# Gated linear attention on Trainium2: score strips of 32 x 32 in place of 64 x 64 for the diagonal and five levels

## The chip, the cores and the metric

The kernel runs on one core of one Trainium2 chip. The metric is the device time of one execution in microseconds (us). Times of a kernel are the median of several executions; the profile comes from one more execution with its own time.

The engines are named as the profile names them: PE (TensorE's matmuls), PEld (TensorE's weight loads), DVE (VectorE), ACT (ScalarE), POOL (GpSimd) and SP (SyncE, which here issues DMAs).

## The reference, cut to what matters

The program is a two-layer backbone over 1024 latent tokens and 256 context tokens. The first layer has neighbourhood attention and mLSTM heads; the second has 16 heads of gated linear attention, run forwards and backwards over the tokens. The change is in the second layer. What one direction of one head computes is, for chunks of the sequence:

```python
b = jnp.cumsum(lfc, axis=2)                       # logs of the decays, per key dimension
o = jnp.einsum('bhtk,bhkv->bhtv', qc * jnp.exp(b), S)
pair = jnp.exp(jnp.where(tri, b[:, :, :, None, :] - b[:, :, None, :, :], -jnp.inf))
a = jnp.einsum('bhtk,bhtsk->bhts', qc, pair * kc[:, :, None, :, :])
o = o + jnp.einsum('bhts,bhsv->bhtv', a, vc)
S = jnp.exp(bL[:, :, 0])[..., None] * S + jnp.einsum('bhsk,bhsv->bhkv', kc * jnp.exp(bL - b), vc)
```

The score `a` of a query t and a key s is a sum over 128 key dimensions, each with its own product of decays between s and t. Layer outputs are normalized per head, gated and projected.

## The kernel before

The kernel has stages in this order: the first layer's input projections, attention, mLSTM and output projection; then the second layer's projections; then from about 2170 to 3165 us the 16 heads, one after another; then the output projection.

**The scores of a head.** The kernel cuts the 1024 tokens into 8 blocks of 128 and computes the scores inside a block for both directions together, into one matrix A of 128 keys by 128 queries a block (`gA`, [128, 8, 128]). It works up through levels. At level `lev` (0 to 6, with h = 2^lev) pairs of neighbouring groups of h tokens meet: keys of one group with queries of the other. `gK` and `gQ` hold keys and queries, each in two copies for the two directions, multiplied with the decays up to the edge of their present group; `gF` (later `gT`) holds each group's total decay. Per level, in `hg_level` (L1450 to L1495):

- ACT copies the right half of each pair's keys out of `gK` into `gksel` (L1466), which has one buffer;
- DVE multiplies `gK` with the neighbour's total decay (`update(K, ...)`, the multiply at L1461);
- PE computes the level's products (L1431, through `strip`);
- DVE multiplies `gQ` in the same way (L1461), and then the totals of two groups into one (L1488);
- the product is merged into the running scores `gD`.

**Strips.** A product isn't made for the whole block of 128 by 128. Up to level 5 a pair of groups lies within 64 tokens, so only the two 64 x 64 squares on a block's diagonal hold anything. `strip` (L1429) computes one of them: all 128 key dimensions, 64 keys as the stationary operand in half of the array's columns (`tile_position=(0, b * 64)`), 64 queries moving. A level has 16 strips, two for each of the 8 blocks. The operands are fp32, and the trace shows each strip as two weight loads and two matmuls. Results are [128, 8, 64] in a PSUM bank (tag `s`, four buffers in this stage).

**Merging.** The diagonal's strips (in `hg_intra`, products of `gkn` and `gq`) are multiplied by a mask into `gD` ([128, 8, 64], L1406). Levels 0 to 5 are merged by a predicated copy under the level's mask (`self.lmask`, L1490). Level 6 joins the two halves of a block; ACT then copies the `gD` squares into A's diagonal squares (L1494) and level 6's result into the other two (L1495). `hg_scan` (L1527 to L1529) uses A with the values.

**What else runs between the levels.** PE fills the time between the trains of strips with the projection of the head's values and gates (`hg_vz`, the dense products of L131 to L133 into `mm`), the transposes of the previous head's output (`hg_out`, L1580), and the context's state (`hg_ctx`: DVE at L1351 to L1357, PE at L1362 and L1372).

**What sets the order.** The kernel is written in program order and a planner with a simulated timeline orders each engine's instructions. `urgent()` gives the level's steps priority over the rest. `seg()` makes PE's pieces follow one another as written (`issue_after(self.last_pe.ins)`), so PE's order is fixed by hand; DVE's and ACT's order is the planner's. Weights come on SP's queue, outputs and sums of weights on POOL's; neither is part of a level's steps.

Elsewhere in the kernel two products use narrow columns of the array as well: the modulation's (L265 and L175: four strips of 32 columns with 512 moving) and neighbourhood attention's (L889: two of 64).

Of the kernel before, what the change touches and what calls it, by code (L numbers as in the profile page):

```python
# [10 lines left out]
F32 = mybir.dt.float32  # L11
F32R = mybir.dt.float32r
U8 = mybir.dt.uint8
AF = mybir.ActivationFunctionType
ALU = mybir.AluOpType
# [4 lines left out]
P = 128  # L20
D = 1024
KD = D // P
LAT = 1024
CTX = 256
SQ = 256
T = LAT + CTX
NT = T // P
# [18 lines left out]
class Prog:  # L46
# [1336 lines left out]
    def hg_intra(self, h, st, pool, prev):  # L1383
        nc = self.nc
        F, q = st["F"], st["q"]
        K = self.t(pool, [P, 2, LAT], F32, "gK", 1)
        nc.vector.tensor_scalar(out=K, in0=F, scalar1=-1.0, scalar2=1.0, op0=ALU.mult, op1=ALU.add)
        if h == 0:
            self.Q = self.t(pool, [P, 2, LAT], F32, "gQ", 1)
        Q = self.Q  # L1390
        ks = [self.t(pool, [P, 512], F32, "gkn", 4) for _ in range(2)]
        halves = [(hf, slice(hf * 512, (hf + 1) * 512)) for hf in (1, 0)]
        with self.urgent():
            for hf, s in halves:
                nc.vector.tensor_tensor(out=ks[hf], in0=K[:, 0, s], in1=K[:, 1, s], op=ALU.add)
            for hf, s in halves:
                for d in range(2):
                    nc.vector.tensor_tensor(out=Q[:, 1 - d, s], in0=q[hf], in1=F[:, d, s], op=ALU.mult)
        hv = dict(Q=Q, K=K, T=F, D=self.t(pool, [P, 8, 64], F32, "gD", 1))
        pa = self.ps("s", [P, 8, 64])  # L1400
        with self.urgent(), self.seg():
            for c in range(8):
                for b in range(2):
                    o = c % 4 * P + b * 64
                    m = self.strip(pa[:, c, :], b, ks[c // 4][:, o : o + 64], q[c // 4][:, o : o + 64])
        nc.vector.tensor_tensor(  # L1406
            out=hv["D"], in0=pa, in1=self.lmask[:, 0, :].unsqueeze(1).to_broadcast([P, 8, 64]), op=ALU.mult
        )
        self.last_pe = m
        tiles = self.hg_vz(st, pool)  # L1410
        for lev in range(7):
            if lev == 6:
                hv["A"] = self.t(pool, [P, 8, P], F32, "gA", 1)
            self.hg_level(hv, lev, pool)
            if lev in (1, 2) and prev:
                prev(lev)
            if lev == 3:
                ctx = self.hg_ctx(st, pool)
                next(ctx)
            if lev == 4:  # L1420
                S = next(ctx)
                if prev:
                    prev(3)
            next(tiles)
        next(tiles)
        return hv, S


    def strip(self, out, b, lhsT, rhs):  # L1429
        s = slice(b * 64, (b + 1) * 64)  # L1430
        return self.nc.tensor.matmul(out[s], lhsT=lhsT, rhs=rhs, start=True, stop=True, tile_position=(0, b * 64))  # L1431


    def hg_close(self, H, hf, pool):
# [14 lines left out]
    def hg_level(self, H, lev, pool):  # L1449
        nc = self.nc  # L1450
        n, h = LAT, 1 << lev
        nb = n // (2 * h)
        K, Q, A, D, Tt = H["K"], H["Q"], H.get("A"), H["D"], H["T"]

        pick = lambda t: _skew(t[:, 0, :].rearrange("p (b s i) -> p b s i", s=2, i=h), 2, n)
        out = self.ps("s", [P, 8, 64])

        def update(t, o, step):
            v = bass.AP(t.tensor, t.offset, [list(t.ap[0]), [n + h, 2], [2 * h, nb], [1, h]])
            tot = bass.AP(Tt.tensor, Tt.offset + o, [list(Tt.ap[0]), [step, 2], [2, nb], [0, h]])  # L1460
            nc.vector.tensor_tensor(out=v, in0=v, in1=tot, op=ALU.mult)  # L1461

        with self.urgent():
            if lev < 6:
                ksel = self.t(pool, [P, n], F32, "gksel", 1)
                m = nc.scalar.copy(ksel.rearrange("p (b s i) -> p b s i", s=2, i=h), pick(K))  # L1466
                if lev == 5:
                    self.level = m
                update(K, 1, n - 1)
            for c, b in ((c, b) for c in range(8) for b in range(2)):  # L1470
                with self.seg():
                    o = c * P + b * 64
                    r = out[:, c, :]
                    if lev < 6:
                        r = r.rearrange("p (b s i) -> p b s i", s=2, i=h)
                        lhsT, rhs = ksel[:, o : o + 64], pick(Q)[:, o // (2 * h) : (o + 64) // (2 * h)]
                    else:
                        lhsT = K[:, b, o : o + 64]
                        rhs = Q[:, 1 - b, c * P + (1 - b) * 64 : c * P + (2 - b) * 64]
                    run = self.strip(r, b, lhsT, rhs)  # L1480
            self.last_pe = run
            update(Q, n + 1, -n - 1)
            if lev == 6:
                update(K, 1, n - 1)
            Tv = Tt[:, :, 0 : 2 * nb].rearrange("p d (b s) -> p d b s", s=2)
            if lev == 6:
                H["T"] = self.t(pool, [P, 2, nb], F32, "gT", 1)
            nc.vector.tensor_tensor(out=H["T"][:, :, 0:nb], in0=Tv[:, :, :, 0], in1=Tv[:, :, :, 1], op=ALU.mult)  # L1488
        if lev < 6:
            nc.vector.copy_predicated(D, self.lmask[:, lev + 1, :].unsqueeze(1).to_broadcast([P, 8, 64]), out)  # L1490
            return
        for b in range(2):
            s, e = slice(b * 64, (b + 1) * 64), slice((1 - b) * 64, (2 - b) * 64)
            nc.scalar.copy(A[s, :, s], D[s])  # L1494
            nc.scalar.copy(A[s, :, e], out[s])  # L1495

    def hg_states(self, st, H, d, c0, c1):
        v = st["v"]
# [98 lines left out]
    def build(self):  # L1597
        tc, nc, a = self.tc, self.nc, self.a
        dma = nc.sync.dma_start
        with ExitStack() as es:  # L1600
# [25 lines left out]
            def load(name, shape, eng=nc.gpsimd):  # L1626
# [12 lines left out]
                out=self.hnc[:, 1, :], in0=self.hnc[:, 0, :], scalar1=-1.0, scalar2=None, op0=ALU.mult  # L1639
# [5 lines left out]
                out=self.qkn, in0=qkn[:, 0:1], scalar1=qkn[:, 1:2], scalar2=0.125, op0=ALU.mult, op1=ALU.mult  # L1645
# [11 lines left out]
            for i in range(2):  # L1657
# [6 lines left out]
                out=self.lb[:, 1, :], in0=self.lb[:, 0, :], scalar1=-1.0, scalar2=1.0, op0=ALU.mult, op1=ALU.add  # L1664
# [16 lines left out]
            with self.pp.phase(ad=2, e=2), tc.tile_pool(name="pre", bufs=2) as pool:  # L1681
# [64 lines left out]
                for t0 in range(4, NT, 2):  # L1746
                    mod(t0, t0 + 2)
                    if t0 == 6:
                        hm, lm = self.h_last
# [75 lines left out]
            lk = self.fp = l1.enter_context(tc.tile_pool(name="hgk", bufs=1))  # L1825
            self.ntw = 1
            with tc.tile_pool(name="op0", bufs=2) as op, ExitStack() as wl:
# [14 lines left out]
                    later = later[2:]  # L1842
                self.zero = self.t(lk, [P, CTX], F32, "gzero", 1)
                nc.vector.memset(self.zero, 0.0)
                self.lmask = self.t(lk, [P, 7, 64], U8, "glm8", 1)
                lm = self.t(op, [P, D], F32, "nx", 1)[:, 0 : 7 * P].rearrange("p (l f) -> p l f", f=P)
                dma(out=lm, in_=a["glm"])
                for b in range(2):
                    s = slice(b * 64, (b + 1) * 64)
                    nc.vector.tensor_copy(self.lmask[s, 0, :], self.ident[s, s])  # L1850
                    nc.vector.tensor_copy(self.lmask[s, 1:7, :], lm[s, 0:6, s])
                self.gate_bc(0, op, 2, 0)
                ys = [self.out_y(4, q, self.yd, op, 4) for q in range(2)]
                wr.close()
# [31 lines left out]
            with l1:  # L1886
# [20 lines left out]
                with tc.tile_pool(name="sx", bufs=1, side="right", reuse_waits="tile") as tp, self.pp.phase(x=4):  # L1907
# [4 lines left out]
                pool, wzp, wv, st = pools  # L1912
                pool = _Two(
                    pool, wzp, l1.enter_context(tc.tile_pool(name="hg", bufs=2, reuse_waits="tile")),
                    ("gq", "gK", "gQ", "gkn", "gksel"), ("wzl", "wzh"),
                )
                for t, n, f in (
                    ("gv", 2, NT * P), ("gz", 1, LAT), ("gEc", 1, 2 * CTX), ("gD", 1, 512), ("gknc", 1, 512), ("gS0", 8, P), ("gS1", 8, P),
                    ("gA", 1, LAT), ("gF", 1, 2 * LAT), ("gFc", 1, 2 * CTX), ("wraw", 3, 512), ("gyt", 1, 512),
                    ("gss", 2, 4), ("gT", 1, 16),  # L1920
                ):
                    for _ in range(n):
                        self.t(pool, [P, f], F32, t, n)
# [62 lines left out]
                for i, k in enumerate((0, 4)):  # L1986
                    raw8 = self.t(pool, [P, 512], F32, "wraw", 3)
                    dma(
                        out=raw8.rearrange("p (j t) -> p j t", j=4),
# [5 lines left out]
                w = block(W[0:D, 0:512], wr * 4 + wo * 4, None, ([pool, 3, "wraw"],) * 7 + ([pool, 1, "gyt"],))  # L1995
# [4 lines left out]
                w = block(self.sw[1], wo * 4 + wr * 4)  # L2000
# [46 lines left out]
            with tc.tile_pool(name="op1", bufs=2) as op, ExitStack() as wl, tc.issue_after(w5_dma.ins):  # L2047
# [26 lines left out]
                e = self.t(wl1, [P, 4, 512], F32, "oe", 1)  # L2074
# [137 lines left out]
def _skew(ap, dim, extra):  # L2212
    a = [list(x) for x in ap.ap]
    a[dim][0] += extra
    return bass.AP(ap.tensor, ap.offset, a)
# [90 lines left out]
```

## Time and profile before

| | us |
|---|---|
| median of three runs | 3311.36 |
| lowest and highest | 3306.84, 3313.35 |
| the profiled execution | 3313.05 |
| its span, first to last instruction | 3311.3 |

| engine | busy, us | share of the span |
|---|---|---|
| PE | 3252.1 | 98% |
| PEld | 2899.0 | 88% |
| DVE | 2217.8 | 67% |
| ACT | 1456.0 | 44% |
| POOL | 797.7 | 24% |

In the trace a row of the timeline is: start, duration, engine, line, operation, the tile written and those read, shape (partitions x elements, for PE active rows * columns ahead of it), the number of instructions merged into the row, and in brackets the idle time ahead of it with what ended it. A row of several matmuls lasts from the first start to the last end. Rows of groups give minimum, median and maximum duration in ns, or the busy time and the mean. The list of waits says who waited for whom: us in total, times, the longest. The share of an engine over the whole span is a mean over stages; here only the stage of the heads matters.

### The profile page before, as it was taken

The page shows a single profiled execution, that of the slowest core. Times are in us where ns is not written, and L with a number is a line of the kernel's source. Part 1 is how long each engine was busy: PE and PEld are TensorE (multiplying, and loading weights), DVE is VectorE, ACT ScalarE, POOL GpSimd, SP SyncE. Part 2 cuts the span into 40 slices and gives each one's busy share as a digit, 9 for nine tenths or more (in the row PEclk, how much of TensorE's full clock was granted, in tenths as well). Part 3 has the DMA queues.
Part 4 walks back from the last instruction along what each step waited for, and adds up shares of the span by engine and source line. Part 5 has one row for each costly group of instructions (what it writes and reads, how often), then busy time and mean ns, then how long its engine had stood idle before and what let it go on. Part 6 is the DMA issues. An engine that isn't in the chain of part 4 may idle for free.

```text
span 3311.3 us, 64736 instructions
## 1 busy us (share of the span) xinstructions
PE 3252.1 (98%) x24746; PEld 2899.0 (88%) x24746; DVE 2217.8 (67%) x5005; ACT 1456.0 (44%) x3396; POOL 797.7 (24%) x1191
## 2 busy tenths in 40 slices
PE   7999999999999999999999999999999999999999
PEld 6799899988989888898878788899999999999977
DVE  5847666666655566687767755577778678677756
ACT  5245554455544444455446333333433433433443
POOL 2222222222211112211110233312332333333210
PEclk9999999999999999999999999999999999999999
DMA  7713222232233434444653233322322324334376
GB/s 238 259 50 86 86 71 81 68 94 84 73 90 103 145 111 123 131 139 147 204 175 114 94 105 105 99 80 76 115 83 92 115 83 111 94 86 103 91 218 167
DMA packets 338103, 379.81 MB, mean 115 GB/s; under 512 B 34601, under 2 KB 269801, under 8 KB 336769
## 3 DMA queue, kind: packets, MB, share of 16 engines
q1 hardware_dynamic: 286032, 236.73, 24.3%
q0 software_dynamic: 51760, 138.94, 13.4%
q8 instruction: 195, 3.19, 0.4%
q14 instruction: 116, 0.94, 0.1%
HBM read 272.31 MB, written 103.08 MB: 113 GB/s over the span
## 4 chain that ended last, share of the span: by engine, by line
PE 82%; DMA 6%; issue 4%; DVE 4%; ACT 2%; POOL 1%; SPq 1%; POOLq 0%; ACTq 0%; DVEq 0%
PE mm L131 15%; PE mm L132 15%; PE mm L133 15%; PE s L1431 4%; PE acc L889 2%; PE tr L869 2%; PE x L131 2%; PE x L132 2%; PE x L133 2%; PE mm L951 2%; PE mm L953 2%; PE acc L661 2%; PE mm L952 2%; PE s L670 2%; PE s L1502 1%
## 5 line engine op out<-in xcount | busy, mean ns | idle before, releaser
L131 PE MATMUL mm<-wh,hh 128*128 128x256 f32 (+1 forms) x1440 | 445.6, 310 | 2.9 <-ACT wh L73 0.8
L132 PE MATMUL mm<-wl,hh 128*128 128x256 f32 (+1 forms) x1440 | 444.9, 309 | 0.0
L133 PE MATMUL mm<-wh,hl 128*128 128x256 f32 (+1 forms) x1440 | 442.3, 307 | 0.0
L131 PE MATMUL mm<-hh,wh 128*128 128x512 f32 (+1 forms) x1076 | 391.2, 364 | 2.7 <-ACT ev L399 1.6
L132 PE MATMUL mm<-hl,wh 128*128 128x512 f32 (+1 forms) x1076 | 387.1, 360 | 0.7 <-DVE hl L346 0.7
L133 PE MATMUL mm<-hh,wl 128*128 128x512 f32 (+1 forms) x1076 | 386.6, 360 | 0.0
L131 PE MATMUL mm<-wzh,hh 128*128 128x256 f32 x1024 | 294.4, 287 | 0.0
L131 PEld LDWEIGHTS mm<-wh,hh 128*128 128x128 f32 x1440 | 271.5, 189 | 17.4 <-issue 1.0
L133 PE MATMUL mm<-wzh,hl 128*128 128x256 f32 x1024 | 284.0, 277 | 0.0
L132 PE MATMUL mm<-wzl,hh 128*128 128x256 f32 x1024 | 283.9, 277 | 0.0
L132 PEld LDWEIGHTS mm<-wl,hh 128*128 128x128 f32 x1440 | 271.4, 188 | 12.6 <-issue 0.7
L133 PEld LDWEIGHTS mm<-wh,hl 128*128 128x128 f32 x1440 | 271.4, 188 | 11.9 <-issue 0.5
L131 PEld LDWEIGHTS mm<-hh,wh 128*128 128x128 f32 x1076 | 202.7, 188 | 32.8 <-ACT ev L399 3.7
L133 PEld LDWEIGHTS mm<-hh,wl 128*128 128x128 f32 x1076 | 202.3, 188 | 29.8 <-DVE wl L74 0.2
L132 PEld LDWEIGHTS mm<-hl,wh 128*128 128x128 f32 x1076 | 202.8, 188 | 28.6 <-DVE hl L346 1.4
L131 PEld LDWEIGHTS mm<-wzh,hh 128*128 128x128 f32 x1024 | 192.8, 188 | 2.4
L132 PEld LDWEIGHTS mm<-wzl,hh 128*128 128x128 f32 x1024 | 192.7, 188 | 0.0
L133 PEld LDWEIGHTS mm<-wzh,hl 128*128 128x128 f32 x1024 | 192.4, 188 | 0.0
L74 DVE TENSOR_TENSOR wl<-wraw,wh 128x512 fp32r<-128x512 f32 x174 | 118.4, 688 | 60.2 <-ACT wh L73 58.2
L1461 DVE TENSOR_TENSOR gQ<-gQ,gF 128x1024 f32<-128x1024 f32 x112 | 142.5, 1272 | 19.3 <-PE s L1431 19.3
L1466 ACT COPY gksel<-gK 128x1024 f32<-128x1024 f32 x96 | 110.5, 1151 | 100.0 <-DVE gK L1461 38.8
L1461 DVE TENSOR_TENSOR gK<-gK,gF 128x1024 f32<-128x1024 f32 x112 | 139.1, 1242 | 18.5 <-ACT gksel L1466 11.3
(608 smaller groups left out, 8562.3 us busy)
## 6 DMA issues: line engine op xcount, KB each, us to landing
wraw<-in_wab_dram SPq DMA_DIRECT2D x108, 256.0 KB
wraw<-yd SPq DMA_DIRECT2D x92, 256.0 KB
br<-in_wc_dram SPq DMA_DIRECT2D x66, 256.0 KB
md<-ev POOLq DMA_DIRECT2D x60, 256.0 KB, 2.7
wraw<-in_wc_dram SPq DMA_DIRECT2D x120, 128.0 KB
mloz<-md SPq DMA_DIRECT2D x40, 256.0 KB
s<-gyt POOLq DMA_DIRECT2D x36, 256.0 KB, 5.3
adar<-in_wada_dram SPq DMA_DIRECT2D x16, 512.0 KB
```

The source lines that it names most:

```text
L74: nc.vector.tensor_tensor(out=lo, in0=x, in1=hi.bitcast(F32), op=ALU.subtract)
L131: mm(ps, lhsT=lh(k), rhs=rh(k), start=(start and k == 0), stop=False, skip_group_check=skip)
L132: mm(ps, lhsT=lh(k), rhs=rl(k), start=False, stop=False, skip_group_check=skip)
L133: m = mm(ps, lhsT=ll(k), rhs=rh(k), start=False, stop=(stop and k == nk - 1), skip_group_check=skip)
L661: nc.tensor.matmul(num, lhsT=qc[:, j, :], rhs=C[d][:, j, :], start=False, stop=(j == 1))
L670: nc.tensor.matmul(u, lhsT=st["k"][c][:, j * P : (j + 1) * P], rhs=vw, start=True, stop=True)
L869: nc.tensor.transpose(pt[:nk, i, :], pr[:, o : o + nk], self.ident)
L889: m = nc.tensor.matmul(yp[h64], lhsT=v[:, h64], rhs=pTs[hd][:nk, i, :], start=(i == turn[0]), stop=(i == turn[-1]), tile_position=(0, hd * ...
L951: mm(ps, lhsT=yh[k], rhs=w.h(kk), start=(kk == 0), stop=False)
L1431: return self.nc.tensor.matmul(out[s], lhsT=lhsT, rhs=rhs, start=True, stop=True, tile_position=(0, b * 64))
L1461: nc.vector.tensor_tensor(out=v, in0=v, in1=tot, op=ALU.mult)
L1466: m = nc.scalar.copy(ksel.rearrange("p (b s i) -> p b s i", s=2, i=h), pick(K))
```

## The change

The diagonal and levels 0 to 4 are computed in strips of 32 keys by 32 queries, four for each block, at the array's column positions 0, 32, 64 and 96. Up to level 4 a pair of groups lies within 32 tokens, so the 32 x 32 squares hold all there is. Results and `gD` have 32 columns a block in place of 64, the masks too. Levels 5 and 6 keep strips of 64. Level 5 is no longer merged into `gD`: ACT copies its result into A's 64 x 64 diagonal squares, and after that the four 32 x 32 squares of `gD` over them. A is therefore taken at level 5 in place of level 6.

Counted a head: 7 x 16 = 112 strips and 16 more of the diagonal before; 6 x 32 + 2 x 16 = 224 after. DVE has one product and six predicated copies of 512 columns before; one product and five copies of 256 after. ACT has four copies of 64 partitions by 512 columns before; four of these and four of 32 partitions by 256 columns after.

The diff, without the lines that only declare the buffer sizes:

```diff
-        hv = dict(Q=Q, K=K, T=F, D=self.t(pool, [P, 8, 64], F32, "gD", 1))
-        pa = self.ps("s", [P, 8, 64])
+        hv = dict(Q=Q, K=K, T=F, D=self.t(pool, [P, 8, 32], F32, "gD", 1))
+        pa = self.ps("s", [P, 8, 32])
         with self.urgent(), self.seg():
             for c in range(8):
-                for b in range(2):
-                    o = c % 4 * P + b * 64
-                    m = self.strip(pa[:, c, :], b, ks[c // 4][:, o : o + 64], q[c // 4][:, o : o + 64])
+                for b in range(4):
+                    o = c % 4 * P + b * 32
+                    m = self.strip(pa[:, c, :], b, 32, ks[c // 4][:, o : o + 32], q[c // 4][:, o : o + 32])
...
-            if lev == 6:
+            if lev == 5:
                 hv["A"] = self.t(pool, [P, 8, P], F32, "gA", 1)
...
-    def strip(self, out, b, lhsT, rhs):
-        s = slice(b * 64, (b + 1) * 64)
-        return self.nc.tensor.matmul(out[s], lhsT=lhsT, rhs=rhs, start=True, stop=True, tile_position=(0, b * 64))
+    def strip(self, out, b, n, lhsT, rhs):
+        s = slice(b * n, (b + 1) * n)
+        return self.nc.tensor.matmul(out[s], lhsT=lhsT, rhs=rhs, start=True, stop=True, tile_position=(0, b * n))
...
-        out = self.ps("s", [P, 8, 64])
+        w = 32 if lev < 5 else 64
+        out = self.ps("s", [P, 8, w])
...
-            for c, b in ((c, b) for c in range(8) for b in range(2)):
+            for c, b in ((c, b) for c in range(8) for b in range(P // w)):
                 with self.seg():
-                    o = c * P + b * 64
+                    o = c * P + b * w
...
-        if lev < 6:
-            nc.vector.copy_predicated(D, self.lmask[:, lev + 1, :].unsqueeze(1).to_broadcast([P, 8, 64]), out)
+        if lev < 5:
+            nc.vector.copy_predicated(D, self.lmask[:, lev + 1, :].unsqueeze(1).to_broadcast([P, 8, 32]), out)
             return
         for b in range(2):
             s, e = slice(b * 64, (b + 1) * 64), slice((1 - b) * 64, (2 - b) * 64)
-            nc.scalar.copy(A[s, :, s], D[s])
-            nc.scalar.copy(A[s, :, e], out[s])
+            nc.scalar.copy(A[s, :, s if lev == 5 else e], out[s])
+        if lev == 5:
+            for b in range(4):
+                s = slice(b * 32, (b + 1) * 32)
+                nc.scalar.copy(A[s, :, s], D[s])
...
-                self.lmask = self.t(lk, [P, 7, 64], U8, "glm8", 1)
+                self.lmask = self.t(lk, [P, 6, 32], U8, "glm8", 1)
...
-                for b in range(2):
-                    s = slice(b * 64, (b + 1) * 64)
+                for b in range(4):
+                    s = slice(b * 32, (b + 1) * 32)
                     nc.vector.tensor_copy(self.lmask[s, 0, :], self.ident[s, s])
-                    nc.vector.tensor_copy(self.lmask[s, 1:7, :], lm[s, 0:6, s])
+                    nc.vector.tensor_copy(self.lmask[s, 1:6, :], lm[s, 0:5, s])
```

More of the change, by code (lines that the diff above doesn't have):

```diff
@@ L1398, in hg_intra @@
                     nc.vector.tensor_tensor(out=Q[:, 1 - d, s], in0=q[hf], in1=F[:, d, s], op=ALU.mult)
-        hv = dict(Q=Q, K=K, T=F, D=self.t(pool, [P, 8, 64], F32, "gD", 1))
-        pa = self.ps("s", [P, 8, 64])
+        hv = dict(Q=Q, K=K, T=F, D=self.t(pool, [P, 8, 32], F32, "gD", 1))
+        pa = self.ps("s", [P, 8, 32])
         with self.urgent(), self.seg():
             for c in range(8):
-                for b in range(2):
-                    o = c % 4 * P + b * 64
-                    m = self.strip(pa[:, c, :], b, ks[c // 4][:, o : o + 64], q[c // 4][:, o : o + 64])
+                for b in range(4):
+                    o = c % 4 * P + b * 32
+                    m = self.strip(pa[:, c, :], b, 32, ks[c // 4][:, o : o + 32], q[c // 4][:, o : o + 32])
         nc.vector.tensor_tensor(
-            out=hv["D"], in0=pa, in1=self.lmask[:, 0, :].unsqueeze(1).to_broadcast([P, 8, 64]), op=ALU.mult
+            out=hv["D"], in0=pa, in1=self.lmask[:, 0, :].unsqueeze(1).to_broadcast([P, 8, 32]), op=ALU.mult
         )
@@ L1475, in hg_level @@
                         r = r.rearrange("p (b s i) -> p b s i", s=2, i=h)
-                        lhsT, rhs = ksel[:, o : o + 64], pick(Q)[:, o // (2 * h) : (o + 64) // (2 * h)]
+                        lhsT, rhs = ksel[:, o : o + w], pick(Q)[:, o // (2 * h) : (o + w) // (2 * h)]
                     else:
@@ L1479, in hg_level @@
                         rhs = Q[:, 1 - b, c * P + (1 - b) * 64 : c * P + (2 - b) * 64]
-                    run = self.strip(r, b, lhsT, rhs)
+                    run = self.strip(r, b, w, lhsT, rhs)
             self.last_pe = run
@@ L1917, in build @@
                 for t, n, f in (
-                    ("gv", 2, NT * P), ("gz", 1, LAT), ("gEc", 1, 2 * CTX), ("gD", 1, 512), ("gknc", 1, 512), ("gS0", 8, P), ("gS1", 8, P),
+                    ("gv", 2, NT * P), ("gz", 1, LAT), ("gEc", 1, 2 * CTX), ("gD", 1, 256), ("gknc", 1, 512), ("gS0", 8, P), ("gS1", 8, P),
                     ("gA", 1, LAT), ("gF", 1, 2 * LAT), ("gFc", 1, 2 * CTX), ("wraw", 3, 512), ("gyt", 1, 512),
```

## The prediction

> **What bounds the kernel now.** I read the page first, then the list of waits of TensorE, then the timeline of one head (the third, 2290 to 2325 us) engine by engine.
>
> ```profile
> PE 3252.1 (98%) x24746; PEld 2899.0 (88%) x24746; DVE 2217.8 (67%) x5005; ACT 1456.0 (44%) x3396; POOL 797.7 (24%) x1191
> ...
> PE 82%; DMA 6%; issue 4%; DVE 4%; ACT 2%; POOL 1%; SPq 1%; POOLq 0%; ACTq 0%; DVEq 0%
> PE mm L131 15%; PE mm L132 15%; PE mm L133 15%; PE s L1431 4%; PE acc L889 2%; PE tr L869 2%; PE x L131 2%; PE x L132 2%; PE x L133 2%; PE mm L951 2%; PE mm L953 2%; PE acc L661 2%; PE mm L952 2%; PE s L670 2%; PE s L1502 1%
> ```
>
> TensorE is busy nearly all the time and carries 82% of the chain that ended last. The strips (L1431) alone are 4% of that chain, some 130 us, so what they take is paid for. The question is where TensorE is *not* the bound inside a head. From the list of waits of TensorE, in the stage of the heads (2170 to 3165 us):
>
> ```profile
> PE s L1431 <- DVE gQ L1461: 8.2, 16, 0.6
> ```
>
> Sixteen waits for 16 heads: one per head, about half a microsecond, for VectorE's update of gQ. The timeline of TensorE shows which strips wait. A strip train is one level's strips in a row: 16 strips, each an fp32 product in two passes, so x32. The rows are the diagonal and level 0, then levels 2 and 3 and the first strips of level 5.
>
> ```profile
> 2293.86 1.15 PE L1431 MATMUL s<-gq,gkn 128*64 128x64 f32 x32
> 2294.84 1.51 PE L1431 MATMUL s<-gQ,gksel 128*64 128x64 f32 x32
> ...
> 2304.47 1.15 PE L1431 MATMUL s<-gQ,gksel 128*64 128x64 f32 x32 [0.53 <-DVE gQ L1461]
> ...
> 2308.88 1.15 PE L1431 MATMUL s<-gQ,gksel 128*64 128x64 f32 x32
> ...
> 2318.28 0.34 PE L1431 MATMUL s<-gQ,gksel 128*64 128x64 f32 x4
> ```
>
> Level 2 waits, the others don't. What level 2 waits for is VectorE, which works without a gap from the first update of gK to the second update of gQ:
>
> ```profile
> 2294.36 1.23 DVE L1461 TENSOR_TENSOR gK<-gK,gF 128x1024 f32<-128x1024 f32 x1 [0.87 <-ACT gksel L1466]
> 2295.50 1.26 DVE L1356 TENSOR_SCALAR gq<-gFc 128x512 f32<-128x512 f32 x1
> 2296.68 0.68 DVE L1406 TENSOR_TENSOR gD<-s,glm 128x512 f32<-128x512 f32 x1
> 2297.29 1.21 DVE L1461 TENSOR_TENSOR gQ<-gQ,gF 128x1024 f32<-128x1024 f32 x1
> 2298.42 0.72 DVE L1490 COPY_PREDICATED gD<-glm,s 128x512 f32<-128x512 uint8 x1
> ...
> 2301.37 0.68 DVE L1357 TENSOR_TENSOR gq<-gq,gEc 128x512 f32<-128x512 f32 x1
> 2301.98 1.21 DVE L1461 TENSOR_TENSOR gK<-gK,gF 128x1024 f32<-128x1024 f32 x1
> 2303.11 1.21 DVE L1461 TENSOR_TENSOR gQ<-gQ,gF 128x1024 f32<-128x1024 f32 x1
> 2304.25 0.72 DVE L1490 COPY_PREDICATED gD<-glm,s 128x512 f32<-128x512 uint8 x1
> ...
> 2307.11 1.22 DVE L1461 TENSOR_TENSOR gQ<-gQ,gF 128x1024 f32<-128x1024 f32 x1
> ```
>
> The block begins when ScalarE has made gksel of level 0, which hangs on the end of the head before and not on a strip. So up to level 2 the head runs at VectorE's pace. After that gQ is ready ahead of TensorE: at 2308.33 (2307.11 and 1.22) for level 3's train at 2308.88, 0.55 us to spare, and the list has no second wait a head at levels 4 to 6. So from level 2's own train on, a shorter train shortens the head.
>
> **The change, part by part.** *Strips.* Six trains of a head (diagonal, levels 0 to 4) get 32 strips, 64 passes, of 32 columns; levels 5 and 6 keep 16 of 64. The price is the pace of passes, of which the trace has three kinds.
>
> ```profile
> 2339.91 2.28 PE L1502 MATMUL s<-gv,gkn 128*128 128x128 f32 x19
> ```
> ```profile
> L1431 PE MATMUL s<-gQ,gksel x3072: 221/222/273, 2171.7 to 3127.2; 128*64 128x64 f32 x192
> ```
> ```profile
> L1502 PE MATMUL s<-gv,gkn x448: 271/275/377, 2209.5 to 3151.1; 128*128 128x128 f32 x150
> ```
> ```profile
> 29.51 0.64 PE L265 MATMUL ad<-adar,sc 128*32 128x512 f32 x4
> ```
> ```profile
> 29.51 1.92 PE L265 MATMUL ad<-adar,sc 128*32 128x512 f32 x16
> ```
> ```profile
> L265 PE MATMUL ad<-adar,sc x64: 589/617/1062, 14.6 to 41.4; 128*32 128x512 f32 x64
> ```
>
> The present train: (1.15 - 0.222) / 31 = 30 ns from start to start, a round of two strips side by side each 60 ns. With 128 key columns and none beside it: (2.28 - 0.275) / 18 = 111 ns. So a round costs 0.80 ns a key column and some 9 ns: the loading of the keys sets it, not the number of queries (L1502 moves 128 columns and isn't slower for that). For 32 columns the line gives 60 - 32 x 0.80 = 34 ns, if four strips run abreast. That four do is seen at L265: four matmuls of 0.617 us lie within 0.64 us, so they start some 7 ns apart, and sixteen end in 1.92 us. A new train then lasts 15 x 34 + 3 x 7 = 0.53 us between first and last start, against 0.93 now: 0.40 us less each. Bounds: four starts of 7 ns take 28 ns a round, which gives 0.44 us (0.49 less); if a round can close only one load after its last strip has started (60 - 7 = 53 ns for 64 columns, so 27 for 32, after 3 x 7), a round is 48 ns and a train 0.74 us (0.19 less). I take 34, since the two rows that lie on its line differ only in the columns. No row shows a hundred instructions at such a pace; that is the third rival.
>
> A rule of the Trainium skill speaks against this: TensorEngine Tiling (Array Packing), section Instruction Overhead, says that a matmul costs about 60 cycles however few columns it moves, and that no tiling factor should be won from a dimension that is already small. By it a round of 32 queries would be as long as one of 64; that is the second rival's case.
>
> Level 0's train is longer (1.51 us) than the others. I leave it as it is, because nothing hangs on it: it, the diagonal and level 1 lie before level 2's gate. Their three gains, about 1.2 us a head, only lengthen TensorE's wait there.
>
> *VectorE.* gD halves from 512 to 256 columns, in the diagonal's product and five predicated copies; level 5's predicated copy goes. Half-size prices are from rows of another product:
>
> ```profile
> L1490 DVE COPY_PREDICATED gD<-glm,s 128x512 f32<-128x512 uint8 x72 | 52.5, 730 | 0.0
> ...
> L1488 DVE TENSOR_TENSOR gF<-gF 128x512 f32<-128x512 f32 x12 | 8.1, 671 | 0.0
> ...
> L1488 DVE TENSOR_TENSOR gF<-gF 128x256 f32<-128x256 f32 x12 | 4.9, 410 | 0.0
> ```
>
> 256 columns less are 671 - 410 = 0.26 us less. In the gap-free block ahead of level 2 stand one such product and one such copy: the gate opens 0.52 us earlier (0.70 if they halve outright). The other four shorten work with slack. At level 3 the slack becomes 0.55 - 0.40 + 0.26 = 0.41 us, still positive, so levels 2, 3 and 4 hand on their 0.40 each. Levels 5 and 6 give nothing.
>
> *ScalarE.* Level 5 now makes six copies into gA, two from the strips' results and four from gD; level 6 keeps two of its four.
>
> ```profile
> 2321.70 1.25 ACT L1494 COPY gA<-gD 64x512 f32<-64x512 f32 x2 [6.08 <-DVE gF L1488]
> 2322.97 0.37 ACT L1340 COPY gv<-mm 128x256 f32<-128x256 f32 x1
> 2323.24 0.39 ACT L1341 ACTIVATE gz<-mm 128x256 f32<-128x256 f32 x1
> 2323.52 1.17 ACT L1495 COPY gA<-s 64x512 f32<-64x512 f32 x2
> ```
>
> Before: 1.25 + 1.17 = 2.42 us. After: 2 x 1.17 + 4 x 0.37 (the row of 256 columns) = 3.82, 1.4 more. Cost nothing: ScalarE idles 6.08 us ahead of them and level 5's train begins at 2318.28, so some 2.6 us of copies fit before gv at 2322.97, and level 6 has fewer than now. Without that cover 1.4 us a head. The masks' loads (four small copies more, once), the DMAs and the queues of SP and POOL are not touched; the added wait of the four gD copies is for level 4's predicated copy, long done.
>
> *Sum.* 0.52 + 3 x 0.40 = 1.72 us a head, x 16 = 27.5 us. The profiled execution took 3313.05 us (span 3311.3): 3285.5. The median of the three runs is 1.7 us lower, 3311.36: **3284 us**.
>
> **The rivals.** *Second: four abreast bring little.* Rounds of 48 ns give (0.52 + 3 x 0.19) x 16 = 17 us, 3294; rounds of 60 ns leave only VectorE's part, 0.52 x 16 = 8 us, 3303. For it: no train in the trace has rounds under 60 ns. Against it: the line through 60 and 111 ns.
>
> *Third, slower: each pass has a price of its own that abreast strips can't share,* because instructions come at a limited rate. The 30 ns a pass of the present trains would stand under twice the passes: 63 x 30 = 1.89 us a train, 0.96 more. Levels 2 to 4 then cost 2.88 a head; diagonal, level 0 (1.51 - 0.222 = 1.29 now) and level 1 cost 2 x 0.96 + 0.60 = 2.52, of which the wait of 0.53 swallows its part: 2.0. Together 4.9 x 16 = 78 us: 3389. It decides from 63 passes = 0.93 + 0.52 / 3 = 1.10 us, that is 17.5 ns a pass. For it: no row runs below 30 ns over a whole train, and level 0's train, which follows another at once, is the slowest. Against it: the L265 rows start four within 23 ns; 64 against 128 columns differ by what the columns explain.
>
> The Trainium skill states such a floor: TensorE: Matmul & The Clock Gate, section "Wait — 56ns, not 53.3ns?", has no start-to-start under about 25 ns however few the columns. By it, as an estimate, a train would be 63 x 25 = 1.58 us and the kernel some 47 us slower, 3358; the 7 ns between L265's starts speak against it across strips, while no row decides it over a whole train.
>
> *Fourth: no change.* The planner orders ScalarE anew and puts the longer copies ahead of work that TensorE needs at the head's end: 1.4 x 16 = 22 us back, 3306. For it: ScalarE's order is not written by hand; against it, the 6 us of idleness.
>
> **How the numbers follow.** First 58%, second 16%, third 16%, fourth 10%. A measurement of this kernel tells about 0.2%, 6.6 us, from no change. First and second are faster by more: 74%. Fourth is the same: 10%. Third is slower: 16%. Leaving the third out and a little of the fourth, the range ends at 3306. Its lower end: rounds of 28 ns and halved VectorE work, (0.70 + 3 x 0.49) x 16 = 35 us, 3277, and some 5 us more if one of the context's operations (0.68 us each, gq at L1357) leaves the block in a part of the heads: 3272.
>
> **What would show it.** Right: 64 passes a train in about 0.72 us with the last matmul's length, gD's operations at about 0.42 to 0.47 us, a wait for gQ ahead of level 2 that has grown from 0.53 to about 1.2 us, none ahead of levels 3 to 5, a head shorter by 1.7 us. Wrong: a train of 64 passes as long as 1.15 us or longer, a wait that appears at level 3 or after the last level, or a head in which level 2 no longer waits at all.

## The result, and the profile after

After the change the kernel takes 3283.53 us (median of four runs, 3282.71 to 3287.57), before it 3309.10 us (four runs in all, 3306.02 to 3313.35). The ratio is 0.9924 with a 95% interval of 0.9907 to 0.9941: 25.6 us, or 0.76%, faster. The profiled execution of after took 3282.71 us. It and the one of before lie at opposite ends of their runs, so their difference (30.3 us) is larger than that of the medians.

The engines, the first line of the chain, and TensorE's waits in the stage of the heads:

```profile
PE 3213.6 (98%) x27818; PEld 2864.3 (87%) x27818; DVE 2183.9 (67%) x4993; ACT 1481.6 (45%) x3460; POOL 797.8 (24%) x1191
...
PE 80%; DVE 7%; DMA 6%; issue 4%; ACT 2%; POOL 1%; SPq 1%; DVEq 0%; ACTq 0%; POOLq 0%
```
```profile
PE s L1431 <- DVE gQ L1462: 21.5, 16, 1.4
```

TensorE has 3072 more matmuls and as many weight loads, and is busy 38 us less. There are still 16 waits for gQ, one a head, but each is now 21.5 / 16 = 1.3 us, where it was 0.5. On the chain VectorE has gone from 4% to 7%.

How long a head is can be read from level 6's trains, first start to last, in the row of the source line, first before, then after the change:

```profile
L1431 PE MATMUL s<-gQ,gK x512: 221/222/271, 2198.2 to 3131.2; 128*64 128x64 f32 x171
```
```profile
L1431 PE MATMUL s<-gQ,gK x512: 221/222/271, 2194.4 to 3102.6; 128*64 128x64 f32 x171
```

Fifteen heads and one train take 933.0 us before and 908.2 after: some 62.1 and 60.5 us a head, 1.65 us less; times 16 that is 26 us, all of the change of the median. The trains of one head after the change (the timeline of TensorE; diagonal, levels 0, 2 and 3):

```profile
2288.27 0.76 PE L1431 MATMUL s<-gq,gkn 128*32 128x32 f32 x64
2288.99 0.89 PE L1431 MATMUL s<-gQ,gksel 128*32 128x32 f32 x64
...
2298.31 0.75 PE L1431 MATMUL s<-gQ,gksel 128*32 128x32 f32 x64 [1.29 <-DVE gQ L1462]
...
2302.32 0.76 PE L1431 MATMUL s<-gQ,gksel 128*32 128x32 f32 x64
```

Twice the passes, and each train is shorter: 1.15 us became 0.75, level 0's 1.51 became 0.89. VectorE's block ahead of level 2, and where it ends:

```profile
2288.77 1.23 DVE L1462 TENSOR_TENSOR gK<-gK,gF 128x1024 f32<-128x1024 f32 x1 [0.88 <-ACT gksel L1467]
2289.92 1.27 DVE L1356 TENSOR_SCALAR gq<-gFc 128x512 f32<-128x512 f32 x1
2291.10 0.41 DVE L1406 TENSOR_TENSOR gD<-s,glm 128x256 f32<-128x256 f32 x1
...
2296.95 1.21 DVE L1462 TENSOR_TENSOR gQ<-gQ,gF 128x1024 f32<-128x1024 f32 x1
2298.09 0.44 DVE L1491 COPY_PREDICATED gD<-glm,s 128x256 f32<-128x256 uint8 x1
```

From the first update of gK to the copy that follows the second update of gQ the block lasts 9.32 us, against 9.89 before (2294.36 to 2304.25): 0.57 us less. The update of gQ is not the only thing that level 2's train needs: ScalarE's copy of its keys, gksel, waits for the update of gK in the same block and ends at 2298.11, 0.05 us ahead of gQ (2298.16). So it is the whole block that has to get shorter and not its last operation alone.

ScalarE at the end of a head:

```profile
2312.29 1.19 ACT L1495 COPY gA<-s 64x512 f32<-64x512 f32 x2 [4.01 <-PE s L1431]
2313.50 1.65 ACT L1499 COPY gA<-gD 32x256 f32<-32x256 f32 x4
```

The six copies take 2.84 us; ScalarE still idles 4.01 us ahead of them.

### The profile page after: what moved, and what is told of

The parts are those of the page before. It is cut to its first block, busy times and chain, and to the rows that moved or that the text cites. A ratio compares the mean times of both kernels' runs of the same rounds, so it can differ in the third digit from the quotient of the medians.

```text
span 3280.7 us, 70941 instructions
## 1 busy us (share of the span) xinstructions
PE 3213.6 (98%) x27818; PEld 2864.3 (87%) x27818; DVE 2183.9 (67%) x4993; ACT 1481.6 (45%) x3460; POOL 797.8 (24%) x1191
## 4 chain that ended last, share of the span: by engine, by line
PE 80%; DVE 7%; DMA 6%; issue 4%; ACT 2%; POOL 1%; SPq 1%; DVEq 0%; ACTq 0%; POOLq 0%
PE mm L131 15%; PE mm L132 15%; PE mm L133 15%; PE acc L889 3%; PE tr L869 2%; PE s L1431 2%; PE x L131 2%; PE x L132 2%; PE x L133 2%; PE mm L951 2%; PE mm L953 2%; PE mm L952 2%; PE acc L661 2%; PE s L670 2%; PE s L1506 1%
```

## The experiments

Each was timed in the same session as the kernel before, and the ratio is to that. The theory to be tested is the prediction's, with the sizes of the profile after: 0.57 us a head come from VectorE's shorter block, 3 x 0.37 from the trains of levels 2, 3 and 4, together 1.68 (the heads show 1.65), and nothing from the first three trains. Rival A gives all of it to VectorE's halved work, rival B to the strips, all of them alike.

**The strips alone.** VectorE reads the narrow result twice and works at its old width.

```diff
-            out=hv["D"], in0=pa, in1=self.lmask[:, 0, :].unsqueeze(1).to_broadcast([P, 8, 32]), op=ALU.mult
+            out=hv["D"], in0=pa.unsqueeze(2).to_broadcast([P, 8, 2, 32]),
+            in1=self.lmask[:, 0, :].unsqueeze(1).unsqueeze(1).to_broadcast([P, 8, 2, 32]), op=ALU.mult
```

The same in the predicated copies.

> The strips of the change alone: VectorE reads each result twice and keeps gD as wide as before, so its product and predicated copies stay at about 0.7 us. My theory: the gain has two parts, 0.57 us a head from VectorE's shorter block ahead of level 2 and 3 x 0.36 us from the trains of levels 2, 3 and 4. Here only the second is left, 17 us against the kernel before, about 3292; the wait for gQ ahead of level 2 grows to some 1.9 us. Rival A, the strips are worth nothing and VectorE's halved work is all: no change, 3309. Rival B, the strips are all: 3283.

Measured: 3290.16 us against 3309.20, ratio 0.9947 (0.9935 to 0.9960), 19 us faster. VectorE's copies and TensorE's waits:

```profile
L1492 DVE COPY_PREDICATED gD<-glm,s x80: 726/735/750, 2171.7 to 3102.0; 128x512 f32<-128x512 uint8 x80
```
```profile
PE s L1432 <- DVE gQ L1463: 28.6, 27, 1.7
```

The copies are nearly as long as before the change (735 and 730 ns), so this is the strips' part without VectorE's. Rivals A (3309) and B (3283) both lie outside the interval. The waits are longer, 1.7 us at most where 1.9 was expected, and in some heads level 1 waits as well, which makes 27.

**VectorE's part alone.** Strips of 64 everywhere; VectorE takes half of their columns, so half of the scores of each square are left out.

```diff
-        w = 32 if lev < 5 else 64
+        w = 64
...
-            nc.vector.copy_predicated(D, self.lmask[:, lev + 1, :].unsqueeze(1).to_broadcast([P, 8, 32]), out)
+            nc.vector.copy_predicated(D, self.lmask[:, lev + 1, :].unsqueeze(1).to_broadcast([P, 8, 32]), out[:, :, 0:32])
```

The diagonal's strips likewise.

> VectorE's part of the change alone: strips of 64 as before, VectorE takes 32 of their 64 columns (this leaves out half of the scores of each square). My theory: only the block ahead of level 2 gets shorter, 0.57 us a head, of which TensorE's wait ahead of level 2 (0.53 us) can be saved: 8 to 9 us, about 3300 to 3301, and the wait all but gone. Rival A, VectorE's work is all: 3283. Rival B, the strips are all: 3309.

Measured: 3302.90 us against 3309.20, ratio 0.9976 (0.9967 to 0.9985): 6 us faster by the medians, 8 by the ratio. TensorE's list of waits has no row for gQ any more. The 8 to 9 us that were expected lie in the interval (5 to 11 us). The two parts by themselves, 0.53% and 0.24%, add up to the whole change's 0.76%.

**Wide strips ahead of the gate.** The gate is the wait ahead of level 2's train. This run is the change with the first three trains undone.

```diff
-        w = 32 if lev < 5 else 64
+        w = 32 if 2 <= lev < 5 else 64
```

The diagonal too, and VectorE takes half of the columns of these three results, as in the run before.

> As after the change, but the diagonal, level 0 and level 1 have strips of 64 again, of which VectorE takes 32 columns (this leaves out half of the scores of these squares). My theory: their time is hidden by TensorE's wait ahead of level 2, so nothing is lost: 3283 to 3286, and the wait shrinks from 1.36 to about 0.1 us. Rival B, each shorter train pays the same: half of the strips' part is lost, at least 9 us: 3292 or more.

Measured: 3285.13 us, ratio 0.9927 (0.9914 to 0.9941), within 2 us of the whole change. TensorE's waits:

```profile
PE s L1431 <- DVE gQ L1462: 0.4, 1, 0.4
```

The waits of 21.5 us are gone, the time is the same. So half of the shorter trains bought nothing but waiting.

**Without the copies of gD.**

```diff
-        if lev == 5:
-            for b in range(4):
-                s = slice(b * 32, (b + 1) * 32)
-                nc.scalar.copy(A[s, :, s], D[s])
```

This leaves out the scores of the diagonal and of levels 0 to 4.

> As after the change, without ScalarE's four copies of gD into gA at level 5 (this leaves out the scores of the diagonal and of levels 0 to 4). My theory: they lie in ScalarE's idle time and cost nothing: 3282 to 3285. Rival, they delay what TensorE needs at the head's end: up to 4 x 0.40 us a head, 26 us, faster by that: 3258.

Measured: 3281.97 us, ratio 0.9918 (0.9904 to 0.9931), no difference from the change that this can show. The interval leaves room for some 5 us, 0.3 us a head; ScalarE's four copies, 1.65 us a head, cost no more than that, and the rival's 26 us are excluded.

**The context's operations behind the gate.** In VectorE's block four long operations belong to the context's state; the planner puts them there because they are ready. This run queues three of them, 2.0 us in all, behind later updates of gQ, and moves TensorE's context products, with what follows them, two levels on. The fourth (1.27 us, L1356) stays.

```diff
-            if lev == 3:
+            if lev == 5:
                 ctx = self.hg_ctx(st, pool)
                 next(ctx)
-            if lev == 4:
+            if lev == 6:
...
+        with self.tc.issue_after(self.up[2]):
             nc.vector.tensor_tensor_scan(E[:, 0, 0 : CTX - 1][:, ::-1], ...)
+        with self.tc.issue_after(self.up[3]):
             nc.vector.tensor_tensor_scan(E[:, 1, 1:CTX], ...)
...
+        with self.tc.issue_after(self.up[4]):
             nc.vector.tensor_tensor(out=k, in0=k, in1=E, op=ALU.mult)
```

Here `self.up[lev]` is that level's update of gQ.

> As after the change, with three of VectorE's context operations (the two scans, 0.68 and 0.65 us, and the product gq, 0.68 us) queued behind the updates of gQ of levels 2, 3 and 4, and TensorE's context products two levels later, with the sums of weights that follow them. My theory: VectorE's block ahead of level 2 is what hides the gain of the first three trains. It loses 2.0 us, TensorE's wait there (1.36 us a head) goes, and the head gets about 1.3 us shorter: 20 us, about 3263, if levels 3 to 5 keep a little slack on VectorE. Rival, the moved operations make levels 3 to 5 wait instead: 3280 or more, with waits for gQ there.

Measured: 3258.06 us against 3306.06, ratio 0.9854 (0.9838 to 0.9871). This is 48 us faster than the kernel before. It is ahead of the change by 25 us by the medians and by 23 by the ratios, since the kernel before, too, took 3 us less when it was timed beside this run. TensorE's list for the heads no longer has the 21.5 us of waits for gQ, and the block is a good 1.5 us shorter (2285.96 to 2293.70, 7.74 us against 9.32; the timeline of VectorE):

```profile
2285.96 1.23 DVE L1466 TENSOR_TENSOR gK<-gK,gF 128x1024 f32<-128x1024 f32 x1 [0.89 <-ACT gksel L1471]
...
2293.70 0.44 DVE L1495 COPY_PREDICATED gD<-glm,s 128x256 f32<-128x256 uint8 x1
```

The 3263 us that were expected (20 us below the change) lie at the upper end of the interval, which runs from 3253 to 3263 us. No level waits for gQ now, so the rival falls.

**The same move in the kernel before.** The edit is the one above, with wide strips.

> The kernel before, with the same three context operations moved as in the run of the later context. My theory: the operations only cost what TensorE waits ahead of level 2. That is 0.53 us a head with wide strips, so 8 to 9 us are to be had here, about 3298, a third of what the same move gave after the change (25 us). Rival, the move is worth the same whatever the strips: 3281.

Measured: 3299.16 us against 3309.93, ratio 0.9967 (0.9954 to 0.9979), 11 us faster, where 8 to 9 were expected (the interval runs from 7 to 15). The same edit is worth 23 to 25 us after the change and 11 before it.

**The later context with wide strips ahead of the gate.** The run of the later context, with the edit that cost nothing in the third experiment; again half of the scores of these squares are left out.

> The kernel with the later context, with strips of 64 again in the diagonal, level 0 and level 1, of which VectorE takes 32 columns (this leaves out half of the scores of these squares). The same edit cost 2 us with the context in its old place. My theory: without the wait ahead of level 2 nothing hides it: 2 x 0.36 + 0.59 = 1.3 us a head, 21 us, about 3279. Rival, these three trains are hidden by something else too: 3258 to 3262.

Measured: 3280.34 us against 3309.93, ratio 0.9909 (0.9894 to 0.9925). Against the later context with narrow strips that is 22 us slower by the medians and 18 by the ratios, where 21 was the theory and at most 4 the rival. The gain of the first three trains was there all along, behind the wait.

**Strips of 16 keys.** For the pace of instructions, level 3 gets a train more:

```diff
+            if lev == 3:
+                for c, b in ((c, b) for c in range(8) for b in range(4)):
+                    with self.seg():
+                        o = c * P + b * 32
+                        r = out[:, c, :].rearrange("p (b s i) -> p b s i", s=2, i=h)[b * 32 : b * 32 + 16]
+                        self.nc.tensor.matmul(
+                            r, lhsT=ksel[:, o : o + 16], rhs=pick(Q)[:, o // (2 * h) : (o + 32) // (2 * h)],
+                            start=True, stop=True, tile_position=(0, b * 32),
+                        )
```

> As after the change, with one train more ahead of level 3's own: 32 strips of 16 keys by 32 queries into the same bank, overwritten by level 3's strips. Theory: two limits stand close together. Loading sets a round of four at columns / 1.2 + 5 ns, so 32 ns for 32 keys, which the first 32 passes of a train (queued while TensorE waits) show; after these the instructions come only every 8.5 ns a pass, 34 ns a round. Then the passes of 16 keys take 7 ns each at first and 8.5 ns after: 0.45 to 0.5 us for 64, and level 3's own train runs at 8.5 ns throughout, 0.54 us. Rival, loading alone is the limit: rounds of 18 ns for 16 keys, 0.29 us, and 0.50 us for level 3's. Second rival, longer runs of instructions get slower still: above 10 ns a pass in level 3's own train.

Measured in the trace (of a single execution, 3299.66 us, whose time says nothing here). The row of the first 31 passes of 16 keys alone, that of the whole train, and level 3's own train right behind it; for comparison, the first 31 passes of a train of 32 keys after the change (the diagonal's):

```profile
2244.03 0.42 PE L1476 MATMUL s<-gQ,gksel 128*16 128x32 f32 x31
```
```profile
2244.03 0.70 PE L1476 MATMUL s<-gQ,gksel 128*16 128x32 f32 x62
...
2244.58 0.73 PE L1431 MATMUL s<-gQ,gksel 128*32 128x32 f32 x62
```
```profile
L1476 PE MATMUL s<-gQ,gksel x1024: 189/193/203, 2182.8 to 3102.0; 128*16 128x32 f32 x171
```
```profile
2288.27 0.45 PE L1431 MATMUL s<-gq,gkn 128*32 128x32 f32 x31
```

Without the last matmul's 0.19 us, the first 31 passes take 0.23 us from start to start (7.7 ns each), all 62 take 0.51, so the later ones take 9 ns each, though nothing about them differs but their place in the train. Level 3's passes of 32 keys go on at (0.73 - 0.20) / 61 = 8.7 ns. Both rivals fall: loading alone would have made it 18 ns for a round of 16 keys, which took 31 ns at first and 36 later, and level 3's train stays below 10 ns a pass.

Half the keys save hardly anything: 0.51 against 0.53 us for 62 passes, and at a train's start 7.7 ns a pass against (0.45 - 0.20) / 30 = 8.3. So with 32 keys the load of the keys alone does not set the pace. The slower pace further on comes from neither keys nor queries, since passes of the same shape ran faster at the start; that it is the rate at which instructions come is argued, not shown. Nor does this run show what sets the pace of the first 31: the 32 queries are the same in both trains. Over the 124 passes of the two trains it gets no slower than 9 ns.

## Why the prediction was right, point by point

- *What bounds a head.* As put: up to level 2 VectorE's block, after it TensorE. The wide strips ahead of the gate (no loss, no wait) and the same edit without the gate (18 to 22 us lost) show it from both sides.
- *A train's price.* Forecast 0.53 us between first and last start, 0.40 less. Measured 0.75 - 0.19 = 0.56, 0.37 less, 8.9 ns a pass or 36 ns a round of four instead of 34. The number is near, but the reason, that the loading of the keys sets a round and not the number of queries, does not hold. The two rows that I drew the line through have 64 keys with 64 queries and 128 with 128, so they differ in both. Two other rows of the trace before tell the two apart (8 passes each; the first has 128 keys and 2 queries, the second 64 keys and 128 queries, two strips abreast):

```profile
31.37 1.05 PE L273 MATMUL tr<-pick,adarow 128*128 128x2 f32 x8
...
308.69 0.61 PE L889 MATMUL acc<-apT,avc 128*64 128x128 f32 x8
```

  With 2 queries, 128 keys still take (1.05 - 0.25) / 7 = 114 ns from start to start: there the keys set the pace. With 128 queries, 64 keys two abreast take (0.61 - 0.28) / 3 = 110 ns a round in place of 60: there the queries do. In L265's rows, with 32 keys and 512 queries, a round takes (1.92 - 0.64) / 3 = 427 ns. So both cost about the same a column, 0.8 to 0.9 ns, and in these rows the larger of the two decides. The change halves both, which is why the line gave nearly the right round; that is luck, and the line would have failed where only the keys are halved: for 16 keys 34 ns less 16 x 0.80 is 21 ns a round, and the run showed about 33.
- *The rule of the Trainium skill* that no tiling factor is to be taken from a dimension that is already small (TensorEngine Tiling (Array Packing), section Instruction Overhead): this case does not bear it out; from 64 to 32 queries, with four abreast, the train went from 0.93 to 0.56 us.
- *Level 0's train.* I counted no more for it than for the others, 0.40 us; it fell from 1.29 to 0.69 us between starts. It did not matter, as the step said, because it lies ahead of the gate.
- *VectorE.* Forecast 0.52 us, measured 0.57: the operations of 256 columns take 0.41 and 0.44 us, 0.27 to 0.29 less each. By itself it is worth 6 to 8 us, about TensorE's wait of 0.53 us a head.
- *ScalarE.* The cover held. A copy of gD takes 0.40 us and not 0.37; leaving them out changed nothing that can be told.
- *Sum.* 1.72 us a head forecast, 1.65 measured; 3284 against 3283.5 us. So close a hit is partly luck: the trains were mis-sized by 3 x 0.03 one way and VectorE by 0.05 the other, and the runs of one kernel spread by 5 us.
- *Second rival* (rounds of 48 or 60 ns): a round is 36. *Fourth* (ScalarE): fell with the run without copies.
- *Third rival.* In a long train a pass does have a price, 8 to 9 ns, that fewer keys don't lower; it is far from 30, and the point from which it would have decided was 17.5. Whether it is the rate of the instructions is not shown. The floor of the Trainium skill, 25 ns from start to start (TensorE: Matmul & The Clock Gate, section "Wait — 56ns, not 53.3ns?") is not seen between strips in different columns of the array: the trains of after run at 8.9 ns over 63 starts.
- *What was to be seen after.* Trains of 0.72 us (0.75), gD's operations of 0.42 to 0.47 (0.41 to 0.44), a wait ahead of level 2 of 1.2 us (1.3), none behind it.

## What to carry to other kernels

Before an engine's work is made shorter, look for the next wait behind it: here six trains were shortened and three paid, the other three only lengthened a wait, and some 23 us more came from moving 2 us of another engine's ready work out of that block. Work that a planner puts early because it is ready can be what everything waits for; ask of each operation in the block whether anyone needs it there. And a price drawn as a line through two sizes says nothing of what sets it when two dimensions grow together: look for a row in which only one of them differs.

## What the runs showed of the hardware that I had not expected

- In long trains of small strips, four abreast, a weight load with its matmul came every 8.7 to 9 ns, with 16 keys as with 32. The first 31 passes of 16 keys after a pause ran at 7.7 ns.
- A round of strips side by side is bounded from two sides at about the same price a column: 128 keys took 114 ns with 2 queries, and 128 queries took 110 ns with 64 keys.
- Level 0's strips, whose queries are picked one by one from the two copies in gQ, ran at (1.51 - 0.22) / 31 = 42 ns a pass with two abreast, against 30 for the others, and at (0.89 - 0.20) / 63 = 11 ns with four, against 8.9. A round of them thus took 24 ns more than one of the others with 64 queries and some 8 more with 32. That the scattered reads are the cause is not tested.
